# Expert 0's rows of the latent half by a one-hot product from SBUF, the context half gathered early

## The chip, the cores and the metric

One core of a Trainium2 chip runs the whole program. The metric is the device time of one execution in microseconds, inputs and outputs in DRAM. All times below are of the kernel before the change.

## The reference, cut to what matters

Two layers (DEPTH = 2) run over 256 context tokens and 256 latent tokens of 1024 channels; only the latent tokens are the output, so the second layer has no context output. Each layer ends in a mixture of experts:

```python
x_lat = layer_norm(ALPHA * x_lat + g1 * y_lat, ln1_g[l], ln1_b[l])
f_lat = grouped_moe(x_lat * (1.0 + sc2) + sh2, w_router, b_router, w_gate[l], w_up[l], w_down[l])
x_lat = layer_norm(ALPHA * x_lat + g2 * f_lat, ln2_g[l], ln2_b[l])
...
def grouped_moe(h, w_router, b_router, w_gate_l, w_up_l, w_down_l):
    ...
    g_idx = jnp.argmax(group_score, axis=-1)                    # one group of 4 experts
    local = lax.top_k(in_grp, TOP_K)[1]                         # the best two in it
    ...
    for e in range(N_EXPERTS):                                  # 16 experts of width 512
        hid = jax.nn.silu(t @ w_gate_l[e]) * (t @ w_up_l[e])
        out = out + combine[:, e:e + 1] * (hid @ w_down_l[e])
```

All of it is fp32.

## The kernel before

Every layer runs the same stages; which instruction stands where on an engine is decided by the framework's scheduler, which goes by the order of the code and by the buffers.

**Output projection** (`w_out`). The two halves of the tokens (hf = 0 context, hf = 1 latent; layer 1 has hf = 1 alone) are projected one after the other. A weight chunk is split on ACT, VectorE and GpSimd into a rounded part `wh` and a remainder `wl` (L411, L412), and three products of the parts make up one fp32 product (L416 to L418). `settle` then adds the statistics of a pair of channel tiles (`stat`) and turns its columns into rows with products against the identity (`tr`, L974).

**Rows of h** (`ln1_end`). The rows that the experts read, h, leave PSUM as four tiles `hr` (128 tokens by 512 channels) and are written to `hD` in DRAM from ACT's queue, each right behind its evacuation (L1114).

**Routing** (`route`). For each half the router's scores give the two experts of each token and its place `q1` in their lists, of at most CAP = 96. Sorting is done with products: VectorE compares `q1` with a row of numbers to one-hot matrices `oh` (L1208), and TensorE multiplies them with the token numbers to `ptb` (L1212); from it come the gather indices `gidx` and the scatter indices (L1216, L1217). In the latent half this runs in four groups of experts, 0 to 1, 2 to 5, 6 to 10 and 11 to 15. `by_load` then sorts experts 3 to 15 by their load: `ids` are their numbers in that order, `gs` their gather indices. Experts 0 to 2 come first always.

**Experts** (`moe`). Each expert takes four weight tiles for gate and up, and two for down, of 1 MB each. They go through 15 slots in turn (7 `we`, 3 `we` that are shared with the projections' weights, 5 `mw`), from SP's queue (`load`, L1314). `gather` brings an expert's rows from `hD` into one of three buffers `xg` by an indirect DMA of GpSimd (L1324), `trans` turns them with eight transposes into `xgT` (L1333), `gu` is the gate-and-up product in two halves of the channels (`pgA` L1348, `pgB` L1358), `down` the other one. The first experts run in this order:

```python
gather(0)
load(0, "gu")
trans(0)
gather(1)
gu(0, k0)
for e in range(2, NXG + 1):
    gather(e)
```

Before the load of a slot whose number is at least NFREE (13 in layer 0, 12 in layer 1) in the first round, GpSimd copies one column of expert 0's gathered rows into it (L1305), so that this load can't start before the gather has landed. From the 16th load on, a load waits until the slot's tile has been used; for experts 3 to 15 SP reads the expert's number into a register first (L1311).

Of the kernel before, what the change touches and what calls it, by code (L numbers as in the profile page):

```python
# [18 lines left out]
P = 128  # L19
D = 1024  # L20
KT = 8
# [15 lines left out]
LN_EPS = 1e-5  # L37
RMS_EPS = 1e-6
IA = 2.0 ** -0.5
NY, NXG = 2, 3  # L40
NADA = 6
NFREE = 13, 12
SPL = ({3: "GVGV", 4: "GGVG", 6: "GGVG", 7: "GGVG", 13: "GVGG", 14: "GVGV"}, {1: "VVGV", 2: "VVGV", 3: "VGVG", 4: "GVGG"})
NF, NTOT, NBT = 1, 1, 3
FILL0 = (0, 0, 0, 2, 2, 2, 2, 0, 2, 0, 2, 2, 0, 2, 0, 2)
# [138 lines left out]
class Emit:  # L184
# [729 lines left out]
    def w_out(self, l):  # L914
# [49 lines left out]
            self.R.update(uv=uv, gbr=gbr)  # L964


        def settle(xs, hf, st, tr, seen):
            self.stat(st, xs, seen)
            for m, x, _ in xs:
                rs = rt([P, 256], "rs", 2)  # L970
                S.activation(rs[:], x, AF.Copy, scale=gb[:, m, 2 * hf:2 * hf + 1])
                for n in range(2):
                    b = 2 * n + m // 4
                    mm(tr[b][:, 128 * (m % 4):128 * (m % 4) + 128], rs[:, 128 * n:128 * n + 128], self.ident,  # L974
                       start=("t", b) not in seen, stop=False, skip_group_check=True)
                    seen.add(("t", b))
# [6 lines left out]
        for half, c in order:  # L983
            if half != hf:
                hf, v = half, 1 - half
                sl = slice(256 * hf, 256 * hf + 256)
                ah, al = [None] * KT, [None] * KT
                for k in ks:
                    if hf == self.halves()[0]:
                        ah[k], al[k] = self.ft([P, NT], f"xh{k}", 1, F32R), self.ft([P, NT], f"xl{k}", 1, F32R)  # L990
                    else:
                        ah[k], al[k] = prev[0][k], prev[1][k]
                    self.split(ah[k][:, sl], al[k][:, sl], self.aT[k // 2][:, k % 2, sl], V)
                prev = (ah, al)
                st = self.bank(2, "st")
                tr = [self.bank(4 + i, "tr") for i in range(4)]
                seen = set()
            if c != last:
                hl, last = self.wsplit(self.A["wout"][l, c], ks[::2], (V, G, V, G)), c
            xs = []  # L1000
            for i in range(2):
                m = 2 * c + i
                ps = self.pa("psy")
                cs = slice(128 * i, 128 * i + 128)
                for k in ks:
                    wh, wl = hl[k // 2]
                    self.mm3(ps[:, 0:256], wh[:, k % 2, cs], wl[:, k % 2, cs], ah[k][:, sl], al[k][:, sl], k == ks[0], k == ks[-1])
                x = self.xk(hf, m)
                V.scalar_tensor_tensor(x, ps[:, 0:256], a[:, 16 + m, v:v + 1], x, op0=ALU.mult, op1=ALU.add)
                xs.append((m, x, w32[:, hf, m, :]))  # L1010
            owed.append((xs, hf, st, tr, seen))
            if len(owed) > 1:
                settle(*owed.pop(0))
            if (half, c) == order[0]:
                rows_of_g()
            if c == order[3 if hf == order[0][0] else -1][1]:
                while owed:
                    settle(*owed.pop(0))
                if hf == 0:
                    self.ln1_end(hf, st, tr)  # L1020
        return st, tr
# [53 lines left out]
    def ln1_end(self, hf, st, tr):  # L1075
# [26 lines left out]
            mm(pr[0:12, 128 * n:128 * n + 128], rows[:, n, :], self.ident, start=True, stop=True, skip_group_check=True)  # L1102
        rT = rt([P, 256], "rT", 1, F32R)
        S.activation(rT[0:12], pr[0:12, 0:256], AF.Copy)
        for n in range(2):
            for j in range(2):
                hr = rt([P, 512], "hr", 4)
                mm(tr[2 * n + j][:], rT[0:12, 128 * n:128 * n + 128], R["gbr"][0:12, 512 * j:512 * j + 512], start=False, stop=True,
                   skip_group_check=True)
                if (n, j) == (1, 0):  # L1110
                    V.tensor_scalar(hr[:], tr[2 * n + j][:], s[:, 3, n:n + 1], None, op0=ALU.mult)
                else:
                    S.activation(hr[:], tr[2 * n + j][:], AF.Copy, scale=s[:, 3, n:n + 1])
                S.dma_start(self.hD[128 * (n0 + n):128 * (n0 + n) + 128, 512 * j:512 * j + 512], hr[:])  # L1114
                if f"h{l}_0" in self.dbg:
                    nc.sync.dma_start(self.dbg[f"h{l}_{n0 + n}"][:, 512 * j:512 * j + 512], hr[:])
# [12 lines left out]
    def route(self, hf, n0, aff):  # L1129
# [60 lines left out]
                mm(ptot, self.one16[:], m16[:, n, :], start=(n == 0), stop=(n == self.T - 1), skip_group_check=True)  # L1190
        q1 = R["q1"][:, ns]
        V.scalar_tensor_tensor(q1, pp[:, :2 * NE].rearrange("p (t e) -> p t e", t=2), 1.0, m16[:, ns], op0=ALU.add, op1=ALU.mult)
        rr = rt([P, 2, NE, 2], "rr", 1, F16)
        tok = self.cst("tok")[:, ns].unsqueeze(2).to_broadcast([P, 2, NE])
        V.tensor_copy(rr[:, :, :, 0], tok)
# [25 lines left out]
                V.tensor_scalar(sums[:CAP, es], pe, float(BIG), None, op0=ALU.add)  # L1221
        if last:
            self.by_load(ptot)

        w3 = rt([P, 2, NE], "w1")
        for i, oh in enumerate((oh1, oh2)):
# [55 lines left out]
    def moe(self, l):  # L1282
# [16 lines left out]
        def load(e, kind, part=None):  # L1299
            t = (wgu if kind == "gu" else wdn).setdefault(e, [])  # L1300
            for i in part or range(4 if kind == "gu" else 2):
                w = self.wslot()
                if NFREE[l] <= self.nslot < NWE + NWP + NMW:

                    G.tensor_copy(w[:CAP, 0, 0:1], xg[0][:CAP, 0:1])  # L1305
                src = self.A["wgu" if kind == "gu" else "wd"]
                if turn[e] is None:
                    src = src[l, e]
                else:
                    if e not in number:  # L1310
                        number[e] = nc.values_load(R["ids"][0:1, turn[e]:turn[e] + 1], engines=(mybir.EngineType.SP,),  # L1311
                                                   min_val=NSTAT, max_val=NE - 1)
                    src = src[l, bass.ds(number[e], 1)].rearrange("o p k c -> (o p) k c")
                nc.sync.dma_start(w, src[:, 2 * i:2 * i + 2, :])  # L1314
                t.append(w)

        def gather(e):
            xg[e] = et([P, D], "xg", NXG)
            if e < NXG:

                G.memset(xg[e][:CAP], 0.0)
            c, r = caps[e], turn[e]
            idx = gidx[:c, e:e + 1] if r is None else R["gs"][:c, r:r + 1]
            G.indirect_dma_start(out=xg[e][:c], out_offset=None, in_=self.hD[:],  # L1324
                                 in_offset=bass.IndirectOffsetOnAxis(ap=idx, axis=0), bounds_check=NTL - 1, oob_is_err=False)

        def trans(e):
            t = xgT[e] = et([P, KT, CAP], "xgT", 2)
# [93 lines left out]
                    self.affine(l, 0, hf, k)  # L1422

        assert T * P == NTL and turn[NE - 1] is not None
        gather(0)
        load(0, "gu")
        trans(0)
        gather(1)
        gu(0, k0)
        for e in range(2, NXG + 1):  # L1430
            gather(e)

        V.tensor_copy(sidx[:CAP], R["sums"][:CAP, :, 1])
# [2 lines left out]
        gu(0, k1)  # L1436
        flag = self.rt([P, 1], "flag", 1, I32)
        for e in range(NE):
            if e + NXG + 1 < NE:
                gather(e + NXG + 1)  # L1440

            early = l == 1 and e == NE - 2
            if e + 1 < NE:
# [183 lines left out]
    def finish(self):  # L1627
# [3 lines left out]
        for n, y in enumerate(self.zt):  # L1631
# [6 lines left out]
                V.scalar_tensor_tensor(z[:, cs], ps[:], self.glast[:, 0, n:n + 1], z[:, cs], op0=ALU.mult, op1=ALU.add,  # L1638
                                       accum_out=st[:, j:j + 1])
            V.tensor_scalar(st[:, 2:3], st[:, 0:1], st[:, 1:2], -1.0 / D, op0=ALU.add, op1=ALU.mult)  # L1640
            sq = self.ep.tile([P, D], F32, tag="xg", bufs=NXG, name="sq")
            S.activation(sq[:], z, AF.Square, bias=st[:, 2:3], accum_out=st[:, 3:4])
            V.tensor_scalar(st[:, 4:5], st[:, 3:4], 1.0 / D, LN_EPS / 2, op0=ALU.mult, op1=ALU.add)
            G.tensor_tensor(st[:, 5:6], st[:, 4:5], self.neghalf[:, 0:1], op=ALU.pow)
# [103 lines left out]
```

## Time and profile before

| | |
|---|---|
| three timed runs | 1319.32, 1322.42, 1322.50 us (median 1322.42) |
| profiled execution | 1320.44 us, span 1318.6 us |
| TensorE busy | 1202.1 us (91%) |
| TensorE weight loads | 754.5 us (57%), beside the matmuls |
| VectorE, ACT, GpSimd busy | 591.8, 413.1, 336.8 us |
| DMA | 338.29 MB, mean 257 GB/s |

The span is the time from the first to the last instruction in the trace; the rest of an execution's time lies around it. The share of busy time is a mean over stages: the experts of layer 0 run from about 450 us, those of layer 1 from about 1060 us.

### The profile page before, as it was taken

To read this page: it belongs to the slowest core of one execution; us is meant where nothing else is said; L and a number is where in the kernel's file an instruction comes from. 1 tells how busy PE (TensorE), PEld (TensorE's weight loads), DVE (VectorE), ACT (ScalarE), POOL (GpSimd) and SP (SyncE) were. 2 spreads that over 40 slices of the span, in tenths; PEclk is the share of its full clock that TensorE was granted. 3 is DMA by queue.
4 is the path that set the end of the run, shared out by engine and by line. 5 is a ranking of instruction groups with operands and counts; after the bars stand their busy time and mean duration, and the time that the engine had idled before them with its cause. 6 is when DMAs were issued, how large, how long until landed. Compare 5 with 4: busy or idle time off the path is not lost. (4 is left out here: it accounts for less than half of the span.)

```text
span 1318.6 us, 23124 instructions
## 1 busy us (share of the span) xinstructions
PE 1202.1 (91%) x9079; PEld 754.5 (57%) x9079; DVE 591.8 (45%) x1397; ACT 413.1 (31%) x905; POOL 336.8 (26%) x350
## 2 busy tenths in 40 slices
PE   6989999999999799999995999989889899999974
PEld 4778777678788344333332588877667734333321
DVE  2466654776735424121111756365885524322214
ACT  2233354453544113111112653344345312011001
POOL 2124233332324101111000534353342311111001
PEclk9999999999999699999997999999999889999996
DMA  8784424313384699999998524244425799999994
GB/s 303 239 294 184 151 93 173 135 48 105 111 324 175 238 372 372 390 392 397 409 420 320 213 100 175 105 188 156 136 91 229 291 331 387 397 409 410 421 420 159
DMA packets 66597, 338.29 MB, mean 257 GB/s; under 512 B 9939, under 2 KB 16819, under 8 KB 30768
## 3 DMA queue, kind: packets, MB, share of 16 engines
q1 hardware_dynamic: 52928, 314.69, 61.7%
q0 software_dynamic: 5936, 12.58, 2.9%
q10 hardware_dynamic: 7616, 9.44, 2.3%
q8 instruction: 75, 1.23, 0.4%
q14 instruction: 42, 0.34, 0.1%
HBM read 321.75 MB, written 20.45 MB: 260 GB/s over the span
## 5 line engine op out<-in xcount | busy, mean ns | idle before, releaser
L412 POOL TENSOR_TENSOR wl<-w,wh 128x512 fp32r<-128x512 f32 x121 | 166.5, 1391 | 193.2 <-ACT wh L411 181.4
L1348 PE MATMUL pgA<-we,xgT 128*64 128x512 f32 x688 | 165.6, 611 | 3.4 <-DMA we<-in_wgu_dram 2.7
L416 PE MATMUL pscm<-xh,wh 128*128 128x512 f32 (+1 forms) x320 | 118.6, 375 | 3.2 <-ACT wh L411 2.3
L417 PE MATMUL pscm<-xl,wh 128*128 128x512 f32 (+1 forms) x320 | 119.8, 377 | 1.0 <-POOL xl L1582 0.8
L418 PE MATMUL pscm<-xh,wl 128*128 128x512 f32 (+1 forms) x320 | 117.3, 371 | 2.8 <-POOL wl L412 2.7
L411 ACT ACTIVATE wh<-w 128x512 fp32r<-128x512 f32 x160 | 97.0, 627 | 62.3 <-PE pscm L417 17.8
L1348 PEld LDWEIGHTS pgA<-we,xgT 128*64 128x64 f32 x688 | 47.3, 139 | 91.3 <-issue 80.5
L417 PE MATMUL pstm<-wl,xh 128*128 128x256 f32 x320 | 92.4, 290 | 3.4 <-DVE wl L412 1.8
L1385 PE MATMUL pdA<-we,hdT 128*64 128x512 f32 x368 | 87.9, 609 | 4.9 <-DMA we<-in_wd_dram 3.2
L418 PE MATMUL pstm<-wh,xl 128*128 128x256 f32 x320 | 92.2, 288 | 0.0
L416 PE MATMUL pstm<-wh,xh 128*128 128x256 f32 x320 | 92.1, 288 | 0.0
L1412 POOL DMA_INDIRECT yD<-y,ss x25 | 23.0, 920 | 247.2 <-DVE y L1400 87.9
L1348 PE MATMUL pgA<-mw,xgT 128*64 128x512 f32 x336 | 77.8, 597 | 1.9 <-DMA mw<-in_wgu_dram 1.9
L1339 DVE COPY xgT<-ptx 128x256 f32<-128x256 f32 (+1 forms) x32 | 15.4, 482 | 132.2 <-PE ptx L1333 93.4
L416 PEld LDWEIGHTS pscm<-xh,wh 128*128 128x128 f32 x320 | 60.5, 191 | 14.5 <-ACT wh L411 2.4
L1366 DVE SCALAR_TENSOR_TENSOR hid<-hid,pgA 128x256 f32<-128x256 f32 x32 | 13.5, 421 | 122.7 <-ACT hid L1365 122.5
L418 PEld LDWEIGHTS pscm<-xh,wl 128*128 128x128 f32 x320 | 61.0, 192 | 12.4 <-POOL wl L412 3.4
L417 PEld LDWEIGHTS pscm<-xl,wh 128*128 128x128 f32 x320 | 61.2, 191 | 11.9 <-POOL xl L1582 1.6
L1365 ACT ACTIVATE hid<-pgA 128x256 f32<-128x256 f32 x32 | 12.3, 384 | 169.2 <-PE pgA L1348 169.2
L417 PEld LDWEIGHTS pstm<-wl,xh 128*128 128x128 f32 x320 | 61.7, 193 | 4.6 <-POOL wl L412 2.2
L416 PEld LDWEIGHTS pstm<-wh,xh 128*128 128x128 f32 x320 | 61.8, 193 | 0.6 <-issue 0.2
L418 PEld LDWEIGHTS pstm<-wh,xl 128*128 128x128 f32 x320 | 61.8, 193 | 0.4 <-issue 0.2
(394 smaller groups left out, 2363.5 us busy)
## 6 DMA issues: line engine op xcount, KB each, us to landing
we<-in_wgu_dram SPq DMA_DIRECT2D x86, 1024.0 KB, 12.0
we<-in_wd_dram SPq DMA_DIRECT2D x46, 1024.0 KB, 15.0
mw<-in_wgu_dram SPq DMA_DIRECT2D x42, 1024.0 KB, 10.7
w<-in_wada_dram SPq DMA_DIRECT2D x41, 1024.0 KB, 7.2
w<-in_win_dram SPq DMA_DIRECT2D x29, 1024.0 KB, 6.1
mw<-in_wd_dram SPq DMA_DIRECT2D x18, 1024.0 KB, 13.3
w<-in_wout_dram SPq DMA_DIRECT2D x11, 1024.0 KB, 4.8
wa<-in_wada_dram SPq DMA_DIRECT2D x6, 1024.0 KB, 21.5
```

The source lines that it names most:

```text
L411: self.nc.scalar.activation(hi, src, AF.Copy)
L412: leng.tensor_tensor(lo, src, hi.bitcast(F32), op=ALU.subtract)
L416: mm(out, lh, rh, start=first, stop=False, **k)
L417: mm(out, lh, rl, start=False, stop=False, **k)
L418: mm(out, ll, rh, start=False, stop=last, **k)
L1339: V.tensor_copy(t[:, 0:4, :c], src)
L1348: mm(pA[64 * j:64 * j + 64, :], xgT[e][:, k, 0:64], wk[:, 512 * j:512 * j + 512], start=(k == 0), stop=(k == KT - 1), skip_group_check=Tru ...
L1365: S.activation(h, ps[:, :n], AF.Tanh, scale=0.5)
L1366: V.scalar_tensor_tensor(h, h, 1.0, ps[:, :n], op0=ALU.add, op1=ALU.mult)
L1385: mm(dA[64 * j:64 * j + 64, :], hdT[e][:, kb, 0:64], wk[:, 512 * j:512 * j + 512], start=(kb == 0), stop=(kb == 3), skip_group_check=True, ...
L1412: G.indirect_dma_start(out=self.yD[l][:], out_offset=bass.IndirectOffsetOnAxis(ap=idx, axis=0), in_=y[:c], in_offset=None, bounds_check=2 ...
```

## The change

Expert 0 is no longer gathered as one list. Of the latent half its rows are picked by a one-hot matrix `oh0` (tokens by places, VectorE, out of the same `q1`), which TensorE multiplies with the four `hr` tiles that still stand in SBUF; the product is the transposed matrix that the expert needs. In layer 0 the context half's rows of expert 0 are gathered early, when the context half has been routed, into `xg0`, and come in by a product with the identity; layer 1 has no context half. Gather 0, its transposes and GpSimd's one-column copies are gone. Gather buffers are two in layer 0 and three in layer 1. `settle` takes a list, does all statistics and then all turns, and the four writes of `hr` are issued behind all four evacuations.

```diff
-NY, NXG = 2, 3
+NY = 2
+NXG = 2, 3
-NFREE = 13, 12
...
-        def settle(xs, hf, st, tr, seen):
-            self.stat(st, xs, seen)
+        def settle(jobs):
+            for xs, hf, st, tr, seen in jobs:
+                self.stat(st, xs, seen)
+            for job in jobs:
+                turns(*job)
+
+        def turns(xs, hf, st, tr, seen):
             for m, x, _ in xs:
...
-                while owed:
-                    settle(*owed.pop(0))
+                settle(owed)
+                owed = []
...
                     S.activation(hr[:], tr[2 * n + j][:], AF.Copy, scale=s[:, 3, n:n + 1])
+        for n in range(2):
+            for j in range(2):
+                hr = hrs[2 * n + j]
                 S.dma_start(self.hD[128 * (n0 + n):128 * (n0 + n) + 128, 512 * j:512 * j + 512], hr[:])
...
+        if last:
+
+            R["oh0"] = rt([P, 256], "rs", 2)[:, :2 * CAP].rearrange("p (n c) -> p n c", n=2)
+            V.tensor_tensor(R["oh0"], self.iota16[:].unsqueeze(1).to_broadcast([P, 2, CAP]),
+                            q1[:, :, 0:1].to_broadcast([P, 2, CAP]), op=ALU.is_equal)
...
         if last:
             self.by_load(ptot)
+        else:
+
+            idx = rt([P, 1], "gidx0", 1, I32)
+            V.tensor_copy(idx[:CAP], sums[:CAP, 0:1, 0])
+            R["xg0"] = rt([P, D], "xg0")
+            G.memset(R["xg0"][:CAP], 0.0)
+            G.indirect_dma_start(out=R["xg0"][:CAP], out_offset=None, in_=self.hD[:CTX],
+                                 in_offset=bass.IndirectOffsetOnAxis(ap=idx[:CAP, 0:1], axis=0), bounds_check=CTX - 1, oob_is_err=False)
...
-                if NFREE[l] <= self.nslot < NWE + NWP + NMW:
-
-                    G.tensor_copy(w[:CAP, 0, 0:1], xg[0][:CAP, 0:1])
...
-            xg[e] = et([P, D], "xg", NXG)
-            if e < NXG:
+            xg[e] = et([P, D], "xg", NXG[l])
+            if e <= NXG[l]:
...
+        def first():
+            t = xgT[0] = et([P, KT, CAP], "xgT", 2)
+            for hf in range(2):
+                pt = self.bank(4 + hf, "ptx")
+                for i in range(4):
+                    terms = [(R["hr"][2 * n + hf][:, 128 * i:128 * i + 128], R["oh0"][:, n]) for n in range(2)]
+                    if l == 0:
+                        terms.insert(0, (R["xg0"][:CAP, 512 * hf + 128 * i:512 * hf + 128 * i + 128], self.ident[:CAP, :CAP]))
+                    for j, (a, b) in enumerate(terms):
+                        mm(pt[:, CAP * i:CAP * i + CAP], a, b, start=(j == 0), stop=(j == len(terms) - 1), skip_group_check=True)
+                src = pt[:, :4 * CAP].rearrange("p (k c) -> p k c", k=4)
+                if hf:
+                    S.activation(t[:, 4:8, :], src, AF.Copy)
+                else:
+                    V.tensor_copy(t[:, 0:4, :], src)
...
-        gather(0)
         load(0, "gu")
-        trans(0)
+        first()
         gather(1)
```

Three places show what moves. On TensorE, in layer 0, the end of the latent half's sort and the start of expert 0 stand like this before (`rr` are the token numbers, `xg_4702` expert 0's gathered rows, `one_103` a constant of ones for a small flag, and `we` a weight slot):

```order
L1212 LDWEIGHTS oh
L1212 MATMUL ptb<-rr_4611,oh 96x2
L1333 MATMUL ptx<-ct,xg_4702 128x96 x8
L1502 LDWEIGHTS one_103
L1502 MATMUL pfl<-fl_0_5359,one_103 128x1
L1348 MATMUL pgA<-we,xgT_4715 64x512 x8
L1358 MATMUL pgB<-we,xgT_4715 32x256 x16
```

And after the change, at the start of the same sort (`rs_4618` is `oh0`, `hr_4556` and `hr_4562` are the first halves of the channels of the two latent token tiles, `xg_0_4159` the early-gathered rows):

```order
L1358 MATMUL ptx<-rs_4618,hr_4556 128x96
L1358 MATMUL ptx<-rs_4618,hr_4562 128x96
L1227 LDWEIGHTS oh
L1227 MATMUL ptb<-rr_4620,oh 96x2
L1358 MATMUL ptx<-ct,xg_0_4159 128x96
L1227 LDWEIGHTS oh
L1227 MATMUL ptb<-rr_4620,oh 96x2
```

The products of expert 0 now stand between the sorting products, two ahead of the first of them and the rest among them, and behind the last sorting product `pgA` follows at once. Two of the 24 products stand further ahead, behind the four products that end in `hr`.

On SP, in layer 0, these are the rows behind the first loads, before (`ids_4676` holds the sorted expert numbers; the two ISA rows belong to the register load ahead of them):

```order
L1314 DMA mw<-in_wgu_dram 128x2048 x3
L1311 TENSOR_LOAD ids_4676
L1311 ISA x2
L1311 TENSOR_LOAD ids_4676
L1311 ISA x2
L1311 TENSOR_LOAD ids_4676
L1311 ISA x2
L1311 TENSOR_LOAD ids_4676
L1311 ISA x2
L1314 DMA mw<-in_wgu_dram 128x2048
L1314 DMA mw<-in_wd_dram 128x2048
L1314 DMA we<-in_wd_dram 128x2048
```

And after the change:

```order
L1334 DMA mw<-in_wgu_dram 128x2048 x4
L1334 DMA mw<-in_wd_dram 128x2048
L1331 TENSOR_LOAD ids_4685
...
L1331 TENSOR_LOAD ids_4685
L1331 ISA x2
L1334 DMA we<-in_wd_dram 128x2048
```

All five `mw` loads stand ahead of the register loads now; of these there are six in a row, where there were four, and behind them is the first load that waits for a slot of expert 0.

On GpSimd, in layer 0, these are the rows around the context half's routing, before (`wl` are the remainders of the projection's weights, `lnst` the statistics of the normalisation):

```order
L412 TENSOR_TENSOR wl_3943<-w_42_3928,wh_3942 128x512
L1054 TENSOR_TENSOR lnst_4038<-lnst_4038,neghalf 128x2
L412 TENSOR_TENSOR wl_4246<-w_43_4239,wh_4245 128x512
L412 TENSOR_TENSOR wl_4254<-w_43_4239,wh_4253 128x512
L412 TENSOR_TENSOR wl_4332<-w_44_4325,wh_4331 128x512
```

And after the change:

```order
L412 TENSOR_TENSOR wl_3943<-w_42_3928,wh_3942 128x512
L1059 TENSOR_TENSOR lnst_4038<-lnst_4038,neghalf 128x2
L412 TENSOR_TENSOR wl_4253<-w_43_4246,wh_4252 128x512
L1245 DMA xg_0_4159<-hD,gidx_0_4157 96x1024
L412 TENSOR_TENSOR wl_4261<-w_43_4246,wh_4260 128x512
L412 TENSOR_TENSOR wl_4339<-w_44_4332,wh_4338 128x512
```

The early gather stands between two remainders of one weight chunk. Its memset (`L1244 MEMSET xg_0_4159 96x1024`) stands at the start of the output projection, ahead of the first remainder and the router's small products. In layer 1 the table of row numbers that the end of the kernel needs (a DMA `rs<-in_const`) moved on SP from the switch to the experts to near the end of their loads, since `oh0` takes that buffer.

## Rows read from the trace of the kernel before

**Rows 1.** Busy time by window: window, length, PE PEld DVE ACT POOL, clock, DMA, GB/s.

```profile
445.00:450.00 5.00, 3.15 (x18) 2.11 (x19) 3.89 (x25) 0.49 (x1) 1.95 (x4) 0.50 0.29 88
```

**Rows 2.** Timeline of TensorE, layer 0: start, duration, instruction, idle before and its releaser.

```profile
444.51 0.88 PE L1212 MATMUL ptb<-rr,oh 128*96 128x2 f16 x10 [0.89 <-DVE sums L1217]
445.81 1.51 PE L1333 MATMUL ptx<-ct,xg 96*128 96x96 f32 x8 [0.42 <-DMA xg<-hD,gidx]
448.93 6.10 PE L1348 MATMUL pgA<-we,xgT 128*64 128x512 f32 x16 [0.60 <-DVE xgT L1339]
```

**Rows 3.** Timeline of TensorE, layer 0, a settle and expert 1.

```profile
420.48 1.16 PE L974 MATMUL tr<-ct,rs 128*128 128x128 f32 x8
456.83 0.88 PE L1333 MATMUL ptx<-ct,xg 96*128 96x96 f32 x8
457.64 3.65 PE L1348 MATMUL pgA<-we,xgT 128*64 128x512 f32 x16
```

**Rows 4.** Timeline of layer 1's switch, three engines.

```profile
1048.30 1.09 DVE L1208 TENSOR_TENSOR oh<-iota,q 128x192 f16<-128x192 f16 x3
1053.54 0.88 PE L1212 MATMUL ptb<-rr,oh 128*96 128x2 f16 x9 [0.41 <-DVE oh L1208]
1058.78 4.97 PE L1348 MATMUL pgA<-we,xgT 128*64 128x512 f32 x16
1058.80 0.82 SPq L1314 DMA_DIRECT2D mw<-in_wgu_dram  x2
1064.81 0.33 SPq L1314 DMA_DIRECT2D we<-in_wd_dram  x1
```

**Rows 5.** Timeline of SP's queue, layer 0.

```profile
449.89 0.33 SPq L1314 DMA_DIRECT2D mw<-in_wgu_dram  x1
456.10 0.33 SPq L1314 DMA_DIRECT2D we<-in_wd_dram  x1
```

**Rows 6.** Busy time by window in both layers' experts, columns as in rows 1.

```profile
512.00:516.00 4.00, 4.00 (x28) 1.18 (x24) 0.57 (x2) 0.28 (x1) 0.00 (x0) 1.00 0.89 296
1120.00:1124.00 4.00, 4.00 (x34) 1.45 (x28) 1.08 (x4) 0.28 (x1) 0.00 (x0) 1.00 0.80 279
```

**Rows 7.** The chain of waits, a stretch near the end.

```profile
1274.48 17.93 DMA we<-in_wd_dram
```

**Rows 8.** Timeline of VectorE, layer 0's switch.

```profile
439.26 1.09 DVE L1208 TENSOR_TENSOR oh<-iota,q 128x192 f16<-128x192 f16 x3
445.43 0.16 DVE L1216 TENSOR_TENSOR gidx<-ptb,sums 96x5 int32<-96x5 f32 x1 [0.63 <-PE ptb L1212]
447.11 0.16 DVE L1258 CAST ids<-idf 128x13 int32<-128x13 f32 x1
```

**Rows 9.** Timeline of GpSimd and TensorE around layer 0's output projection.

```profile
358.88 1.30 POOL L412 TENSOR_TENSOR wl<-w,wh 128x512 fp32r<-128x512 f32 x1
360.51 0.28 PE L418 MATMUL psy<-xh,wl 128*128 128x256 f32 x1
425.30 0.95 POOL L1321 MEMSET xg<- 96x1024 f32 x1 [3.09 <-PE psy L418]
```

**Rows 10.** Timeline of VectorE and GpSimd, the context half's sort.

```profile
399.36 4.50 DVE L1208 TENSOR_TENSOR t<-iota,q 128x1536 f16<-128x1536 f16 x2
400.17 4.82 POOL L412 TENSOR_TENSOR wl<-w,wh 128x512 fp32r<-128x512 f32 x2 [6.77 <-ACT wh L411]
```

**Rows 11.** The gather buffers xg: landing times, and two gathers of layer 0.

```profile
598.27 0.98 POOL L1324 DMA_INDIRECT xg<-hD,gs  x1 [3.19 <-PE ptx L1333]
622.21 0.94 POOL L1324 DMA_INDIRECT xg<-hD,gs  x1 [9.38 <-PE ptx L1333]
...
DMA to landing us min/median/max: 4.1/7.5/9.5
```

**Rows 12.** The write of h: timeline of ACT's queue, and DMA issues (KB, us to landing).

```profile
438.67 0.33 ACTq L1114 DMA_DIRECT2D hD<-hr  x1
...
hD<-hr ACTq DMA_DIRECT2D x12, 256.0 KB, 2.2
```

More of the change, by code (lines that the diff above doesn't have):

```diff
@@ L1012, in w_out @@
             if len(owed) > 1:
-                settle(*owed.pop(0))
+                settle([owed.pop(0)])
             if (half, c) == order[0]:
@@ L1016, in w_out @@
             if c == order[3 if hf == order[0][0] else -1][1]:
-                while owed:
-                    settle(*owed.pop(0))
+                settle(owed)
+                owed = []
                 if hf == 0:
@@ L1104, in ln1_end @@
         S.activation(rT[0:12], pr[0:12, 0:256], AF.Copy)
+        R["hr"] = hrs = []
         for n in range(2):
@@ L1107, in ln1_end @@
                 hr = rt([P, 512], "hr", 4)
+                hrs.append(hr)
                 mm(tr[2 * n + j][:], rT[0:12, 128 * n:128 * n + 128], R["gbr"][0:12, 512 * j:512 * j + 512], start=False, stop=True,
@@ L1424, in moe @@
         assert T * P == NTL and turn[NE - 1] is not None
-        gather(0)
         load(0, "gu")
-        trans(0)
+        first()
         gather(1)
         gu(0, k0)
-        for e in range(2, NXG + 1):
+        for e in range(2, NXG[l] + 1):
             gather(e)
@@ L1438, in moe @@
         for e in range(NE):
-            if e + NXG + 1 < NE:
-                gather(e + NXG + 1)
+            if e + NXG[l] + 1 < NE:
+                gather(e + NXG[l] + 1)
             early = l == 1 and e == NE - 2
@@ L1640, in finish @@
             V.tensor_scalar(st[:, 2:3], st[:, 0:1], st[:, 1:2], -1.0 / D, op0=ALU.add, op1=ALU.mult)
-            sq = self.ep.tile([P, D], F32, tag="xg", bufs=NXG, name="sq")
+            sq = self.ep.tile([P, D], F32, tag="xg", bufs=NXG[1], name="sq")
             S.activation(sq[:], z, AF.Square, bias=st[:, 2:3], accum_out=st[:, 3:4])
```

## The prediction

> **What bounds the kernel now.** I read the busy times by window first, then the timelines of the engines at the two places where a layer goes from its router to its experts, then the DMA queue, then the chain that ended last.
>
> The reader is to see two kinds of stage. In the expert stage TensorE works without a pause and the DMA engines are full. In the switch before it TensorE waits in short steps for VectorE and for one gather, at a clock of 0.50, the lower of its two levels [rows 1]. In layer 0's switch the last small sorting product (ptb) starts at 444.51, expert 0's gathered rows let TensorE begin its transposes at 445.81, and the first gate-and-up product starts at 448.93 [rows 2]. That piece takes 6.10 us for 16 records; a later one at the full clock takes 3.65 [rows 3]. With a pace of 3.65 above and 7.3 below, 6.10 means that the clock rose 4.9 us after 448.93. So the first half of expert 0 is done at 455.03. Layer 1 looks alike: start at 1058.78, 4.97 us, done at 1063.75 [rows 4]; the same sum puts the rise 2.6 us after its start, 4.2 us after the transposes ahead of it.
>
> The weight loads are the other half. There are 15 slots. In layer 0 the 14th is filled only from 449.89, and the next load waits for expert 0 to give a slot back, at 456.10 [rows 5]; in layer 1 three slots are filled from 1058.80 and the first is given back at 1064.81 [rows 4]. From there the engines are near full, with one kind of exception: 0.89 busy in 512 to 516 and 0.80 in 1120 to 1124 [rows 6]. There the loads had caught up with the slots, so TensorE set the pace of the loads. The chain of work that ended last runs over loads in the second half of layer 1's experts; its last load begins to hold it at 1274.48 [rows 7].
>
> **What is taken away.** Per layer: the gather of expert 0 and its eight transposes between the sort and the first product, and GpSimd's one-column copies that held two (layer 0) or three (layer 1) slots back until that gather had landed.
>
> **What is added on the path, layer 0.** VectorE makes one more 128x192 comparison, and makes it first: three of them take 1.09 us, so 0.36 [rows 8]. It is ready at 439.62, and TensorE can begin at about 439.7. From there 22 products of 96 columns stand between the 32 ptb pairs (two more, of the gathered rows, stand ahead of the comparison in an idle stretch), and the first expert product behind all of them. Price of one: a transpose of 96 columns is 0.88/8 = 0.11 at the full clock [rows 3] and 1.51/8 = 0.19 at the lower [rows 2]. A true fp32 product gives two records: the four tr products of a settle are eight records of 1.16/8 = 0.145 for 128 columns [rows 3], so 0.29 a product, and 0.22 for 96 columns. Floor of the unknown: one record, 0.11; I take two, since tr is the same kind of instruction: 0.22 full, 0.38 at the lower clock. A ptb pair costs 0.88/10 [rows 2], 2.8 us for 32.
> All at the lower clock: 439.7 + 22 x 0.38 + 2.8 = 450.9. All at the full clock: 439.7 + 4.8 + 2.8 = 447.3. The work is dense now, where before it had gaps of VectorE's length; in the two dense stretches above the clock rose 4.9 and 4.2 us in, so I put the rise here 4.5 us in, at 444.2. Of the 11.2 us of slow work 6.7 are left then, 5.0 of it products that shrink to 2.9: the end is 444.2 + 2.9 + 1.7 = 448.8. The copies to SBUF lie beside the last ptb group. The first half of expert 0 then runs at the full clock: 448.9 + 3.65 = 452.55, against 455.03. **Gain 2.5**, with bounds of a gain of 4.0 (full clock all along) and a loss of 2.1 (lower clock all along, and then again 6.10).
>
> The Trainium skill, page "TensorE: Matmul & The Clock Gate", section "Terms", gives transposing a mode that is four times faster for FP32, which speaks against putting products in place of transposes. The rows above show 0.29 to 0.11, or 2.6 for more columns, and 2 for the same; by the page's factor the product would cost 0.44, and the sum would be that of the fourth rival below.
>
> **Layer 1.** 16 products, no gathered half. The comparison is ready at 1048.66 [rows 4]; all slow 1048.75 + 6.1 + 2.8 = 1057.65, and with the clock up after 4.5 us 1056.4. Here the last two ptb groups stand behind each other, so VectorE's 0.9 us between them (0.41 waited, and a 480-wide comparison) stays: 1057.3. Then 1057.4 + 3.65 = 1061.05 against 1063.75. **Gain 2.7**, bounds 0.1 and 4.1.
>
> **What that is worth at the end.** Layer 0's experts keep TensorE busy to their end, so 2.5 comes through if the loads follow. They restart later than the slot comes back: the sync engine now has six register loads of expert numbers ahead of the first refill. The numbers were there at 447.27, 1.84 after the last gidx [rows 8], and four loads took until 449.89 [rows 5], 0.65 each. With the last sort at 448.8: 448.9 + 1.84 + 6 x 0.65 = 454.6, that is 1.5 earlier than 456.10. The missing 1.0 is about what the queue stood idle in 512 to 516 and its neighbours [rows 6], so I keep 2.5. In layer 1 three MB are there earlier (7.5 us of loads begun at 1058.80, some 3 us of them unfinished at 1064.81), but the queue ran dry at 1120 to 1124 waiting for TensorE [rows 6], so a head start of the loads ends there and only TensorE's 2.7 goes on to the end of the chain. The prefetch itself I price at nothing; the cover is that dry stretch, and 3.3 us more come if it does not hold.
>
> **What moves elsewhere.** At the start of layer 0's output projection GpSimd gets a memset of 96x1024, 0.95 us [rows 9], ahead of the weight remainder that it finished at 360.18 and that TensorE took at 360.51 [rows 9]: a stall of 0.95 - 0.33 = **0.6**. Behind half 0's sort GpSimd issues the early gather between two remainders. Those two took 4.82 us beside VectorE's one-hot of 4.50 [rows 10]. The second now waits for the gather (about 407.5), and so leaves VectorE alone; TensorE waits for that one-hot, and I take **0.4** off (none to 0.8). The remainder itself is then late by the difference, behind the products that TensorE has from the remainder before it: I cost that at nothing, and if that cover is gone it costs the same 0.4 that the one-hot gives. Two gather buffers in place of three in layer 0: a gather can start when the transposes two experts ahead are done. Gathers two apart start at 598.27 and 622.21, 24 us, and land in at most 9.5 [rows 11]: hidden, with 14 us of cover. The table of row numbers for the very end is loaded late in the stream of layer 1: 0.1 MB, **0.2**.
>
> **Sum.** -2.5 - 2.7 + 0.6 - 0.4 + 0.2 = -4.8 us. The profiled execution took 1320.44 (span 1318.6 and 1.84 around it): 1315.6. The median of the runs shown is 2.0 higher, the lowest run 1.1 lower; against the mean of the four, 1321.2, it is 1316.4, and I give that.
>
> **The rivals.**
> 1. The head start of the loads comes through to the end of layer 1, because the dry stretch is shorter in this order: 3.3 us more, 1313.1. For it: the chain ends on loads [rows 7]. Against it: 0.80 at 1120 [rows 6].
> 2. The products do not bring the clock up (they are short and lie between ptb pairs; the ptb pairs alone, before, did not). Layer 0 loses 2.1, layer 1 gains 0.1, the rest adds 0.4: about 1323.6, no change that can be told.
> 3. Slower: expert 1's gather becomes the late one. Its rows wait for the write of h, issued until 439.0 and landed in 2.2 us before [rows 12], which now meets two or three MB of weights that were held back. If write and gather each take the 9.5 us that gathers take in the full stream [rows 11], with 1 us of issue between, expert 1's rows are there at 459.0; TensorE wants them at 452.55 + 1.9 = 454.5. A wait of 4.5 in layer 0 and about 5 in layer 1 turns the gains into losses of 2.0 and 2.3: with the 0.4, about 1325.9. It decides from 15.5 us for write and gather together. Against it: the held-back loads are at most 7.5 us of work and start well before the write.
>  The Trainium skill, page "DMA: Bandwidth & Descriptors", section "Queues, rings and completion order", says that an engine takes turns between queues, packet by packet, which speaks against a write that waits for a whole stream; no row here shows it directly.
> 4. A product costs four transposes, 0.44 and 0.76: the sort ends at 453.8 and 1061.1, a loss of 2.5 and 1.0, in all 1325.1. Against it: the tr rows.
> 5. The shallower gathering stalls layer 0's experts: 14 us of cover must go; each us beyond costs up to 13 experts a us.
>
> **How the numbers follow.** Chances: forecast 0.58, its own range 1313 to 1320 (half of each bound); rival 1 0.14; rival 2 0.14; rival 3 0.05; rival 4 0.05; rival 5 0.04. About 0.3%, 4 us, is what a measurement of this kernel can tell from no change. The forecast lies only 0.8 beyond it, so I count 0.65 of its chance as faster: 0.38 and rival 1 make 0.52. Same: 0.20 of the forecast, rival 2, and part of the rest, 0.37. Slower 0.11. The range runs from below rival 1 to just short of rival 2: 1311.5 to 1322.5.
>
> **What would show it.** Right: the first gate-and-up records of both layers start near 448.9 (less what the start has lost) and 1057.4 on that layer's own scale and take 3.65; the granted clock rises between 443 and 446; ptx in two records of about 0.1 or 0.19 each; the first refill near 454.6; the queue dry near 1120 again. Wrong: the first records still take 5 to 6 us (rival 2), a wait for xg ahead of expert 1's transposes (rival 3), ptx of four records (rival 4), DMA full throughout in layer 1 (rival 1).

## The result and the profile after

The changed kernel takes 1337.75 us in the median (1335.27 to 1338.77, four runs), against 1322.46 of the kernel before beside it: a ratio of 1.0135, with a 95% interval from 1.0109 to 1.0162. (The ratios here and below are not quotients of the medians; here that quotient is 1.0116, which lies in the interval.) It is slower by 15 us, where 5 us faster was forecast. The profiled execution took 1335.27 us, span 1333.5.

Two places hold the loss, and one of them is not in the prediction at all. It is seen in the waits of the sync engine of after, in 515 to 545 and then in 1120 to 1160 (waited for in total, how often, longest, in us):

```profile
SPq L1541 <- DVE flag L1540: 10.1, 1, 10.1
...
SPq L1541 <- DVE flag L1540: 13.4, 1, 13.4
```

And here is the sync engine's timeline of after around the two waits (start, duration in us, then what is loaded):

```profile
521.09 3.01 SPq L1334 DMA_DIRECT2D we<-in_wd_dram  x2
535.02 2.34 SPq L1334 DMA_DIRECT2D mw<-in_wgu_dram  x4
...
1133.66 3.04 SPq L1334 DMA_DIRECT2D we<-in_wgu_dram  x3
1150.87 0.91 SPq L1334 DMA_DIRECT2D we<-in_wd_dram  x2
```

By the busy time by window, in layer 1 next to nothing moves meanwhile (the last two columns are the share of the DMA engines and GB/s):

```profile
1144.00:1151.00 7.00, 7.00 (x59) 2.55 (x57) 3.33 (x8) 0.00 (x0) 0.86 (x1) 1.00 0.03 9
```

The queue of the weight loads stands still for 10.1 us in layer 0, and for 13.4 in layer 1. What it waits for is a small number, the flag that tells whether an expert has more tokens than places; the sync engine reads it into a register. The next two fences have rows of the views by tile of pfl and of the flag, first of before and then of after: line, engine, operation, count, durations in ns, first and last start.

```profile
L1502 PE MATMUL pfl<-fl,one x2: 184/186/187, 448.2 to 1057.2; 128*128 128x1 f16 x2
L1503 DVE CAST flag<-pfl x2: 146/146/147, 449.0 to 1057.4; 128x1 int32<-128x1 f32 x2
L1504 SPq TENSOR_LOAD <-flag x2: 273/277/281, 492.3 to 1057.6; - x2
```

```profile
L1539 PE MATMUL pfl<-fl,one x2: 177/178/178, 532.2 to 1148.0; 128*128 128x1 f16 x2
L1540 DVE CAST flag<-pfl x2: 158/158/159, 534.0 to 1149.9; 128x1 int32<-128x1 f32 x2
L1541 SPq TENSOR_LOAD <-flag x2: 270/273/276, 534.2 to 1150.1; - x2
```

Before, the one-column product pfl stood in a pause of TensorE ahead of expert 0. It is written in expert 3; the scheduler had put it into that pause. After the change TensorE begins expert 0 (447.60 and 1065.93) before VectorE starts the reduction that pfl needs (450.2 and 1067.6). The product now stands where it is written, 84 us later in layer 0, the cast behind it, and the register load on the sync engine waits in the middle of the weight stream. That the closed pause is what moved it is read off this order; no run tests it.

The second place is the switch itself. It is measured between two rows of TensorE, the products that make rows of h (tr by gbr) and the second half of expert 0 (pgB). Here they are in the kernel before, in layer 0 and in layer 1:

```profile
434.91 2.07 PE L1108 MATMUL tr<-gbr,rT 12*128 12x512 f32 x4 [0.46 <-ACT rT L1104]
454.96 1.93 PE L1358 MATMUL pgB<-we,xgT 128*32 128x256 f32 x32
...
1044.68 1.20 PE L1108 MATMUL tr<-gbr,rT 12*128 12x512 f32 x4 [0.46 <-ACT rT L1104]
1063.68 1.93 PE L1358 MATMUL pgB<-we,xgT 128*32 128x256 f32 x32
```

And here are rows of TensorE's timeline of after in both layers, which answer to these and to [rows 1, 2, 4]:

```profile
430.38 2.07 PE L1115 MATMUL tr<-gbr,rT 12*128 12x512 f32 x4 [0.46 <-ACT rT L1109]
...
435.16 1.17 PE L1358 MATMUL ptx<-rs,hr 128*128 128x96 f32 x4 [0.68 <-DVE rs L1206]
...
438.31 1.06 PE L1358 MATMUL ptx<-rs,hr 128*128 128x96 f32 x4
439.16 0.63 PE L1358 MATMUL ptx<-ct,xg 96*128 96x96 f32 x2
...
446.73 0.93 PE L1227 MATMUL ptb<-rr,oh 128*96 128x2 f16 x10
447.60 6.01 PE L1386 MATMUL pgA<-we,xgT 128*64 128x512 f32 x16
453.54 1.93 PE L1396 MATMUL pgB<-we,xgT 128*32 128x256 f32 x32
...
1049.23 1.67 PE L1115 MATMUL tr<-gbr,rT 12*128 12x512 f32 x4 [0.46 <-ACT rT L1109]
...
1063.88 0.88 PE L1227 MATMUL ptb<-rr,oh 128*96 128x2 f16 x9 [0.40 <-DVE oh L1223]
1065.93 5.76 PE L1386 MATMUL pgA<-we,xgT 128*64 128x512 f32 x16 [1.17 <-issue]
1071.62 1.93 PE L1396 MATMUL pgB<-we,xgT 128*32 128x256 f32 x32
```

And one row of its busy time by window in layer 0 (TensorE's products, its weight loads, VectorE, ScalarE, GpSimd, then the clock, and the DMA columns):

```profile
440.00:444.00 4.00, 4.00 (x28) 4.00 (x27) 1.36 (x4) 0.00 (x0) 1.75 (x2) 0.50 0.07 11
```

The profiled execution of after is 4.5 us ahead before this stage is reached (the clock of before was 0.83 in 20 to 40 us and 0.91 in 60 to 80, that of after 1.00), so the switch has to be measured from a point of its own. In layer 0 it takes 20.1 us before and 23.2 after, in layer 1 19.0 and 22.4. It became 3.1 and 3.4 us longer, where 2.5 and 2.7 shorter was forecast. TensorE has no idle time in 436 to 447.6, its weight loads next to none (4.00 of 4.00 in the row above), and the clock stays at 0.50. It rises only inside the first gate-and-up product, which takes 6.01 and 5.76 us, not 3.65. In layer 1 the clock also fell sooner: the tr products took 1.67 us there, not 1.20, and the first product of expert 0 starts 4.56 us after they start, where the first sorting product started 4.03 after them before.

### The profile page after: what moved, and what is told of

It is laid out like the page before. It is cut to its first block, busy times and chain, and to the rows that moved or that the text cites. A ratio compares the mean times of both kernels' runs of the same rounds, so it can differ in the third digit from the quotient of the medians.

```text
span 1333.5 us, 23238 instructions
## 1 busy us (share of the span) xinstructions
PE 1215.6 (91%) x9143; PEld 767.7 (58%) x9143; DVE 592.7 (44%) x1400; ACT 413.4 (31%) x905; POOL 333.8 (25%) x344
## 5 line engine op out<-in xcount | busy, mean ns | idle before, releaser
L418 PEld LDWEIGHTS pscm<-xh,wl 128*128 128x128 f32 x320 | 61.4, 193 | 12.4 <-POOL wl L412 3.4
## 6 DMA issues: line engine op xcount, KB each, us to landing
mw<-in_wgu_dram SPq DMA_DIRECT2D x42, 1024.0 KB, 15.3
mw<-in_wd_dram SPq DMA_DIRECT2D x18, 1024.0 KB, 20.1
```

Of the source, the lines that this page charges most:

```text
L418: mm(out, ll, rh, start=False, stop=last, **k)
```

## The experiments

Ratios are against runs of the kernel before on the same chip; the medians stand in one table at the end of this section. The kernel before had medians of 1319.61 to 1322.46 us in four such measurements, so medians of different ones can differ by 3 us for no reason of the kernels.

**The flag.** Three kernels ask whether the wait for the flag makes the loss, and whether it is the read on the sync engine. `flag_early` writes the whole flag ahead of expert 1's transposes:

```diff
+        flag = self.rt([P, 1], "flag", 1, I32)
+        fl16 = self.rt([P, 1], "fl16", 1, F16)
+        V.tensor_reduce(fl16[:], R["ov"][:, :T], axis=AX.XY, op=ALU.max)
+        pfl = self.bank(7, "pfl")
+        mm(pfl[:, 0:1], self.one16[:], fl16[:], start=True, stop=True)
+        V.tensor_copy(flag[:], pfl[:, 0:1])
+        fv = nc.values_load(flag[0:1, 0:1], min_val=0, max_val=P)
         trans(1)
         gu(0, k1)
...
-            if e == 3:
-                fl16 = self.rt([P, 1], "fl16", 1, F16)
...
```

> The changed kernel with the overflow flag (its reduction, its one-column product, its cast and the register loads) written ahead of expert 1's transposes instead of in expert 3; nothing else is changed. Theory A (the sync engine's register load of the flag holds the weight queue for 10.1 us in layer 0 and 13.4 in layer 1, and that is most of the loss): no wait for the flag of over 1 us on the sync engine, layer 1's switch begins about 6 us earlier, the whole is 13 us shorter than the changed kernel: about 1324, within 0.3% of the kernel before. Theory B (the products on TensorE and what they do to slots and queue make the loss): the wait only moves to another load, and the time stays at 1333 to 1338.

`flag_read_last` leaves product and cast where the change has them and moves the register load alone:

```diff
-                fv = nc.values_load(flag[0:1, 0:1], min_val=0, max_val=P)
         if l == 0:
...
             self.finish()
+        fv = nc.values_load(flag[0:1, 0:1], min_val=0, max_val=P)
         with self.tc.If(fv):
```

> The changed kernel with the register load of the flag alone moved behind all loads of the layer; the flag's product and cast stay where the changed kernel has them (532 and 534 us in layer 0). Theory A: the gaps in the weight stream at 524 to 535 and 1137 to 1151 are gone and the time is that of flag_early within 3 us, about 1324. Theory A2 (it is the late product or cast on TensorE and VectorE that costs, not the read on the sync engine): 1333 to 1338 as before. Theory B: 1333 to 1338 too.

`before_flag_late` does the reverse in the kernel before:

```diff
-            if e == 3:
+            if e == 4:
...
-                V.tensor_copy(flag[:], pfl[:, 0:1])
+                V.scalar_tensor_tensor(flag[:], xgT[6][:, 0, 0:1], 0.0, pfl[:, 0:1], op0=ALU.mult, op1=ALU.add)
```

> The kernel before with its flag made late: the flag is computed in expert 4, adding zero times a column of expert 6's transposed rows, so that its cast stands on VectorE in the same row as in the changed kernel and its read on the sync engine three rows later in layer 0. Expert 0 is gathered and turned as before. Theory A: a wait for the flag of 5 to 10 us in layer 0 and about 10 in layer 1, time 1330 to 1336, with no product in it. Theory B: no change, 1320 to 1324.

Measured: flag_early 1.0076 (1.0052 to 1.0100), flag_read_last 1.0058 (1.0032 to 1.0085), before_flag_late 1.0124 (1.0085 to 1.0163). Here is the read in the middle of the stream of before_flag_late, from the waits of the sync engine in 500 to 560 and in 1120 to 1170:

```profile
SPq L1504 <- DVE flag L1503: 11.8, 1, 11.8
...
SPq L1504 <- DVE flag L1503: 17.2, 1, 17.2
```

Theory A holds: the late flag alone, with no product in it, makes the old kernel 1.2% slower; and moving the read alone gives as much back as moving all of the flag, though its cast is still at 536.9 us, so it is the read's place in the weight queue, and not the late product or cast. That before_flag_late is as slow as the change is partly chance: its waits are longer (expected were 5 to 10 and about 10), and it has no products. With the read out of the way the loads of layer 0 run through: in flag_early the next `mw` load is 2.9 us behind the end of the pair ahead of it, not 10.9, as these rows of its sync engine show:

```profile
524.40 3.01 SPq L1334 DMA_DIRECT2D we<-in_wd_dram  x2
530.26 10.24 SPq L1334 DMA_DIRECT2D mw<-in_wgu_dram  x4
```

The size was expected too large: 9 to 10 us came back, not 13, and a loss of 0.6 to 0.8% stayed. Theory A alone is not the whole.

**The products against the gather.** `product_undone` is flag_early with gather(0) and trans(0) back in place of first():

```diff
+        gather(0)
         load(0, "gu")
-        first()
+        trans(0)
         gather(1)
```

> flag_early with expert 0 gathered and turned again (gather, eight transposes) in place of the products; no column copies hold slots back, the early gather of the context half is still made but not used, and settle, the order of the writes of h and the two gather buffers of layer 0 stay as in the change. If the products at the low clock cost 2.5 us in layer 0 and 3.4 in layer 1, as the two traces say, this is 4 to 6 us shorter than flag_early, about 1319. If the products cost nothing against the gather, the two are within 2 us. If ungated weight loads delay the gather of expert 0, it is longer than flag_early by that.

It gave 1.0063 (1.0036 to 1.0091), no better than flag_early, and its switch in layer 0 is 23.1 us long as well. But for another reason: a row of its TensorE, layer 0:

```profile
449.07 1.51 PE L1371 MATMUL ptx<-ct,xg 96*128 96x96 f32 x8 [5.55 <-DMA xg<-hD,gidx]
```

The gather is late by 5.5 us, which is 0.42 in [rows 2]. `undone_gated` puts GpSimd's one-column copies back, so that the last two and three slots wait for the gather:

```diff
+NFREE = 13, 12
...
                 w = self.wslot()
+                if NFREE[l] <= self.nslot < NWE + NWP + NMW:
+
+                    G.tensor_copy(w[:CAP, 0, 0:1], xg[0][:CAP, 0:1])
```

> product_undone with GpSimd's one-column copies back: the last two (layer 0) and three (layer 1) slots wait for expert 0's gather again. Theory D (in product_undone the weight loads that were no longer held back delayed the write of h and so the gather: a wait of 5.5 us ahead of the transposes): the wait falls to about 0.5 us, the switch to 20 and 19 us as in the kernel before, the whole to 1321 to 1324. If the wait came from the order of the four writes instead, it stays and the time is 1327 to 1330.

It gave 1.0015 (0.9994 to 1.0036), and the same row of its TensorE:

```profile
445.58 1.51 PE L1375 MATMUL ptx<-ct,xg 96*128 96x96 f32 x8 [0.28 <-DMA xg<-hD,gidx]
```

In layer 1 the wait falls from 4.6 to 0.4 us. Theory D holds, and the traces say which transfer was late: in layer 0 the four writes of h landed 7.5 to 7.9 us after their issue in product_undone and 2.3 to 2.5 in undone_gated, while the gathers took as long in both (medians 4.3 and 4.7). The held-back slots are not all that sets this wait: in three kernels below that are gated too, but without the early gather (small_edits_alone, three_buffers_again, two_buffers_alone), it is 2.5 us in layer 0, with writes that landed in 2 to 2.7; why is open. So the fair partner of the products is the gated gather, and against that the products cost 5.6 us between the medians (1328.91 to 1323.28, on two chips) and 0.6% between the ratios, whose intervals do not meet. By the traces it is 3.6 us in layer 0's switch and 3.2 in layer 1's.

**The clock.** `product_fast_clock` fills TensorE's idle steps ahead of the products with work that nobody reads. It is written behind expert 0's first half, and the scheduler placed it in the pauses (the `fil` rows below):

```diff
+        self.ss = ss
...
         gu(0, k0)
+        fb = self.bank(2, "fil")
+        for _ in range(14):
+            mm(fb[0:64, 0:256], self.ss[:, 0:64], self.ss[:, 0:256], start=True, stop=True, skip_group_check=True)
```

> flag_early with 14 filler products per layer (64 by 256 columns of the statistics tile with itself, into a bank that nobody reads) in TensorE's idle steps between the statistics and the products of expert 0; the output is unchanged. Theory C (the products of expert 0 cost more than the gather they replace because TensorE runs at the lower level there, and short products behind weight loads do not bring it up): if the fillers hold the clock at 1.00, the time from the row products of h to the second half of expert 0 falls from 23.0 to about 17 us in layer 0 and from 22.3 to about 16.5 in layer 1, and the whole to about 1317. Theory C2 (the clock falls all the same in the stretch of short products, whatever stands ahead): 23 and 22 us again, 1328 to 1330.

`before_fast_clock` has 24 of them in the kernel before, with the flag early:

> The kernel before with 24 such fillers per layer and the flag written early; expert 0 is gathered as before. Theory C: the clock stays at 1.00 into the expert stage, expert 0's first half takes 3.65 instead of 6.10 and 4.97 us and its transposes 0.88 instead of 1.5: 3 us less in layer 0 and 2 in layer 1, about 1315. If the fillers stand in the way of the small products (up to 0.5 us at each of six steps), the gain is eaten up and the time stays within 3 us of the kernel before. Theory C2: clock 0.50 as before, 1320 to 1324.

They gave 0.9977 (0.9958 to 0.9996) and 0.9985 (0.9969 to 1.0002). Here are two of layer 0's windows of product_fast_clock, then rows of its TensorE's timeline, then a window of flag_early, which differs by the fillers alone:

```profile
435.00:440.00 5.00, 5.00 (x38) 3.36 (x38) 3.75 (x19) 0.85 (x2) 0.00 (x0) 1.00 1.00 392
440.00:445.00 5.00, 5.00 (x54) 4.70 (x53) 3.61 (x13) 0.29 (x1) 0.10 (x1) 1.00 0.49 189
```

```profile
432.42 1.08 PE L1470 MATMUL fil<-lnss 128*64 128x256 f32 x4
433.42 1.19 PE L1116 MATMUL tr<-gbr,rT 12*128 12x512 f32 x4
...
440.05 0.61 PE L1359 MATMUL ptx<-rs,hr 128*128 128x96 f32 x4
440.50 0.39 PE L1359 MATMUL ptx<-ct,xg 96*128 96x96 f32 x2
...
446.63 3.60 PE L1387 MATMUL pgA<-we,xgT 128*64 128x512 f32 x15
450.16 1.93 PE L1397 MATMUL pgB<-we,xgT 128*32 128x256 f32 x32
```

```profile
444.00:448.00 4.00, 4.00 (x28) 4.00 (x27) 1.37 (x4) 0.00 (x0) 1.84 (x2) 0.50 0.08 16
```

Theory C holds: the clock is 1.00 through the stretch in which it was 0.50, and it does not fall during the products. The switch takes 16.7 us in layer 0 (433.42 to 450.16) and 16.0 in layer 1, 6 less than in flag_early and 3 less than in the kernel before. In before_fast_clock it takes 18.1 and 19.0: layer 0 gains 2.0 and layer 1 nothing, since there seven fillers (3.2 us from 1053.34) stand directly ahead of the transposes: the gathered rows had landed by 1053.84, and the transposes begin at 1056.51.

These two kernels ran beside each other, and they are the comparison of product and gather at the full clock: 1317.52 and 1318.49 us, with intervals that overlap. Without the 2.7 us that the fillers held the transposes back, before_fast_clock's switches would take an estimated 18.1 and 16.3 us, against 16.7 and 16.0. So most of what product_fast_clock gains is the clock's; that the products are worth something of their own is not shown.

**The rest.** `small_edits_alone` takes the early gather, its buffer and the comparison out of undone_gated and has three gather buffers again; `two_buffers_alone` differs from it by `NXG = 2, 3` for `NXG = 3, 3`, and was timed beside a second run of the same kernel, `three_buffers_again`. `product_fast_clock_gated` holds the last slots back as before the change, from expert 0's transposed rows:

```diff
+NFREE = 13, 12
...
+                if NFREE[l] <= self.nslot < NWE + NWP + NMW:
+
+                    G.tensor_copy(w[:, 0, 0:1], xgT[0][:, 0, 0:1])
```

> undone_gated with three gather buffers in layer 0, without the early gather, its buffer and its clearing, and without the comparison for the product: of the change only the order of the statistics and turns, of the evacuations and writes of h are left, and the flag is early. If two gather buffers or the early gather cost the 2.4 us by which layer 0's experts are longer in flag_early, this is 2 to 3 us shorter than undone_gated, and within 2 us of the kernel before. If the order of statistics and writes costs something, it is longer than the kernel before by that.

> small_edits_alone with two gather buffers in layer 0 in place of three, and nothing else. If the second half of undone_gated's loss (about 2 us in layer 0's experts) comes from the shallower gathering, this is 2 to 3 us longer than the three-buffer kernel of the same call; if it came from the early gather or the comparison, the two are within 1 us.

> small_edits_alone once more, as the partner of two_buffers_alone on the same chip. 1319 to 1322, within 0.2% of the kernel before.

> product_fast_clock with the one-column copies back, now from expert 0's transposed rows, so that the last two (layer 0) and three (layer 1) slots are again filled only when expert 0 can start. If the head start of the weight loads is worth nothing, as the prediction took it, this is within 2 us of product_fast_clock, about 1318 to 1320. If it is worth what its bytes are (5 us of loads in layer 0, 7.5 in layer 1, of which 3 were unfinished when a slot came back), it is 3 to 6 us longer, 1321 to 1324.

Measured: 1.0005 (0.9985 to 1.0025) for the small edits, 0.9998 (0.9974 to 1.0022) for the same again, 1.0020 (0.9997 to 1.0042) with two buffers. The new order of statistics, turns and writes costs and brings nothing that can be seen. Two buffers cost 2.2 us between the medians, but the intervals overlap: not shown. The traces do not help. From the second half of expert 0 to the last product of layer 0's experts it is 245.4 us with two buffers and 242.9 in three_buffers_again, but 244.9 in small_edits_alone, which is the same kernel; gathers land as fast (median 7.6 and 7.5 us), and the 2.2 us for which TensorE waits for weight loads at the end of that layer are 1.7 in small_edits_alone. The held-back slots cost nothing clear: 0.9992 (0.9974 to 1.0009) beside 0.9977. In that kernel's trace layer 0's experts take 249.8 us, against 245.3 in product_fast_clock, which is more than the 1.9 by which one kernel differs from itself, so a small price is left open.

| kernel | median us | ratio |
|---|---|---|
| the change | 1337.75 | 1.0135 |
| before_flag_late | 1335.51 | 1.0124 |
| flag_early | 1328.91 | 1.0076 |
| product_undone | 1328.56 | 1.0063 |
| flag_read_last | 1327.57 | 1.0058 |
| undone_gated | 1323.28 | 1.0015 |
| two_buffers_alone | 1323.01 | 1.0020 |
| three_buffers_again | 1320.76 | 0.9998 |
| small_edits_alone | 1320.12 | 1.0005 |
| product_fast_clock_gated | 1319.24 | 0.9992 |
| before_fast_clock | 1318.49 | 0.9985 |
| product_fast_clock | 1317.52 | 0.9977 |

## Why the prediction was wrong

By the medians the change's loss of 15.3 us is made up of some 9 for the flag, 5.6 for the products at the low clock, and the 1.9 by which undone_gated stands above the kernel before, which its interval does not tell from nothing. That is 16.3, within the 3 us by which medians of different measurements are off. By the ratios it is 0.6, 0.6 and 0.15 of 1.35%.

**The flag is missing from the sum.** "The sync engine now has six register loads of expert numbers ahead of the first refill" is where the step failed: the prediction followed the register loads as far as the first refill, and priced them right (0.65 us each; the six begin 0.62 apart, from 449.6 to 452.7), but not the next register load on the same queue, the flag's. That the first refill was forecast for 454.6 and came at 454.67 is luck: after runs 4.5 us ahead there, so on the scale of before it came at 459.2, and it waited last for expert 0's slot (1.4 us, for pgB), not for the register loads.

Nor did it follow TensorE's row pfl, which it had in sight where the change puts expert 0's product directly behind the last sorting product. The instructions that a change moves without touching them have to be traced to whoever waits for them. No rival had this mechanism. The Trainium skill, page "Perfetto Trace Analysis", section "Per-engine timelines", says that an instruction of the sequencer alone waits for its semaphores there, and that the sequencer is free for the next one only afterwards, with the wait not in the profiler's record. The trace agrees: the read has a duration of 0.27 us, and the queue stood still for 10.1.

**The clock did not rise with the products.** "I put the rise here 4.5 us in, at 444.2" failed: 12.4 us of products without a pause did not bring it up, and it rose about 5 us into the wide products behind them. That is the second rival, which had the chance 0.14 and was priced too low: a loss of 2.1 and a gain of 0.1, where the switch grew by 3.1 and 3.4.

In layer 0 22 products and the ptb pairs took 12.4 us (435.16 to 447.60) in place of the 11.2 that were the bound at the low clock: a product took 0.43 there (438.31 and the row behind it begin 0.85 apart, which is 0.21 for each of four records, two to a product), not 0.38, which is less than twice the prediction's own 0.22 at the full clock.

In layer 1 a product took some 0.45, which makes 1.1 us for 16; the first of them came 0.5 us later behind the row products than forecast; and the wide products took 5.76, where the bound let them take 4.97 again. The fourth part is the 1.17 us of idle time ahead of pgA: "The copies to SBUF lie beside the last ptb group" did not hold in layer 1, where VectorE's copy of the first half stands behind its work on the last sort (1065.28, 0.55 us long) and pgA begins 0.1 us after it. Together these are some 3.5 us, which is the step from a gain of 0.1 to a loss of 3.4.

At the full clock the price of 0.22 a product was right to the hundredth (product_fast_clock: 440.05 and the row behind it begin 0.45 apart, four records), and there the switch is 3.3 and 3.0 us shorter than before; but the gather with fillers comes near that (before_fast_clock), so it is the clock's gain in the main.

The Trainium skill, page "TensorE: Matmul & The Clock Gate", section "HAM oscillation — how this bites in real kernels", says that pauses between bursts put TensorE back to its lower level. The rows agree for the fall: in the kernel before TensorE idled for 0.99, 1.15 and 0.46 us in the 4 us ahead of 434.91, and the clock was 1.00 in 430 to 432, 0.86 in 432 to 434 and 0.50 in 434 to 436; fillers in the pauses prevented it. For the rise, 12.4 us without a pause were not enough here; why these products do not bring it is not shown.

**The small terms.** The memset at the start of the output projection stalled TensorE for 0.38 us (forecast 0.6). The 0.4 for less contention did not come: the one-hot of the context half took 4.50 us again. Two gather buffers, priced at nothing for their 14 us of cover, cost 2.2 us between medians, which is not shown to be more than nothing. The prefetch, priced at nothing, is worth nothing that can be told from the times (product_fast_clock_gated). Rival 3 was right that ungated loads delay a gather that stands right behind the write of h, though it is the write that is slow; it looked for that at expert 1, where the trace of after has no such wait, and product_undone shows it at expert 0.

## What to carry to other kernels

When an edit fills an engine's pause, look for what a scheduler had put into that pause, and follow it to its last reader; a value that a DMA queue's engine reads into a register should be computed and read early by hand, or read behind the last load. Products that replace a latency cost what the clock makes of them: price them at the level that the profile shows for that stretch, and if they pay only at the full clock, try spare work in the pauses ahead of them, and try it without the change too. And a throttle on transfers that looks idle may protect a short transfer on the path (here the write of h); once no product waits for that transfer, it may be dispensable.

## What the runs showed of the hardware that was not expected

In flag_early TensorE stayed at the lower of its two levels through 12 us without idle time (three windows of 4 us from 440 on, each busy 4.00 of 4.00 at 0.50; one of them is shown above), with the products of 96 columns and the two-column ptb at work, and its clock rose inside the wide products that followed. In product_fast_clock, where the fillers came first, the same products ran at 1.00 from end to end (440 to 445, weight loads busy 4.70 of 5.00). Fourteen spare products per layer were worth 11 us of median to the changed kernel with its flag early (1328.91 to 1317.52, on two chips; 6.3 and 6.4 us in the switches of the traces). That has the lowest median of all versions run here, 0.23% below the kernel before, with an interval that ends at 0.04%; from before_fast_clock it cannot be told apart.

The write of h, 1 MB in four parts, landed 7.5 to 7.9 us after its issue while weight loads were not held back, and 2.3 to 2.5 us after it where the last two slots waited (product_undone and undone_gated, layer 0).
